# Norming and modulating six of eight first-layer tiles from a second, channel-major copy of the input

## The chip, the cores and the metric

The kernel runs on one core of a Trainium2 chip. The metric is the device time of one launch in microseconds (us), the median of several runs. Before the change three runs took 973.47, 970.46 and 969.55 us, median 970.46 us.

## The reference

Two layers of one mixer each, over 1024 tokens of 1024 channels. Only the head of a layer matters for this change:

```python
def rms_norm(x, gain=None):
    xf = x.astype(jnp.float32)
    y = xf * lax.rsqrt(jnp.mean(xf * xf, axis=-1, keepdims=True) + EPS)
    if gain is not None:
        y = y * gain.astype(jnp.float32)
    return y.astype(x.dtype)

def hybrid_layer(x, c_act, ...):
    mod = c_act @ w_mod + b_mod
    shift, scale, gate = jnp.split(mod[:, None, :], 3, axis=-1)
    h = rms_norm(x, pre_gain) * (1.0 + scale) + shift
    proj = h @ w_in
    ...
    y = jnp.concatenate([a_out, r_out, g_out], axis=-1) @ w_out
    return x + gate * rms_norm(y, post_gain)
```

`proj` is cut into the queries, keys, values and gates of three head groups: windowed attention, retention and gated linear attention. Each token's row of x is divided by its root mean square; each channel is then scaled and shifted.

## The kernel before

**Tiles.** The 1024 tokens are eight tiles of 128. A tile of x is loaded with tokens on partitions, two halves of 128x512. The input projection needs h with channels on partitions, since TensorE contracts over partitions, and in two parts: `hi`, h rounded to the fast 32-bit matmul type, and `lo`, the rest. A projection is 24 products: eight channel blocks, three times (hi by hi, lo by hi, hi by lo), in `accum`. Weights are split in the same way, each unit of 256 columns as four loads of 256 KB into staging buffers, a cast on ScalarE (L488 for the unit `rg`) and a subtraction on VectorE or GpSimd (L491).

**What `pre` does with a tile** of the first layer, from tile 2 on. ScalarE squares both halves and sums (L581). VectorE adds and scales (L534, L528), GpSimd takes the power -1/2 (L529, here "the root"). Both halves are multiplied by the root (L602 on VectorE; L600 on ScalarE for the first half of tiles 2 and 3). TensorE turns them with eight 128x128 transposes by the identity (L176). From PSUM, ScalarE (first half, L622) and VectorE (second half, L624) apply scale and shift, block by block, four each. ScalarE casts each half to `hi` (L628); GpSimd (first half) or VectorE (second half) subtracts for `lo` (L629). Tiles 0 and 1 have a path of their own (`pre_early`), which the change leaves alone.

**Order.** TensorE's order is the program's: generators for each piece of work are resumed by a planner in Python (`pump`, `step`) that keeps a clock of its own and reads latencies from the table `L`. On the other engines and on the DMA queues a scheduler orders the instructions when the program is built; on the chip each engine works its list strictly in order. Almost all loads are issued by SyncE (SP); its eight completion semaphores are used in turn, so a load waits until the eighth load before it has landed.

**Where the change falls.** TensorE's first dense work: the gate unit `gg` for tiles 0 and 1 (272 columns), `rg` for tiles 0 and 1 (256 columns), `gg` for 2 and 3, `rg` for 2 and 3, `gg` for 4 and 5, and so on. Between them stand the transposes of tiles 2 to 7. SyncE at that time loads, in this order: x of tiles 2 and 3, the weights of `rg`, six constants, x of tiles 4 to 7 (L686), small constants, among them the attention sinks (L797, copied by VectorE at L799) and the norm gain `gncol` (L807, scaled by VectorE at L808). VectorE's L1009 finishes the SiLU of a gate after ScalarE's L1007.

The line that the change works on is this one, in `pre`:

```python
            pt = aux()
            for k in range(4):
                transp(pt[:, k * P:(k + 1) * P], xn[j][:, k * P:(k + 1) * P], ident)
```

Of the kernel before, what the change touches and what calls it, by code (L numbers as in the profile page):

```python
# [89 lines left out]
def trunk(ctx: ExitStack, tc: tile.TileContext, ins, cst, out):  # L90
    nc = tc.nc
    V, A, G, T = nc.vector, nc.scalar, nc.gpsimd, nc.tensor
    x_in, c_in, pos_in, w_mod, b_mod, pre_g, post_g, w_in, sinks, gw_in, gb_in, gn_in, w_out = [
        ins[n] for n in _INS
    ]

# [12 lines left out]
    def t2(dt=F32):  # L109
        return gp.tile([P, 512], dt, tag="t2", name=nm("t2"), bufs=B2)  # L110
# [13 lines left out]
    def aux(dt=F32):  # L124
        return ps.tile([P, 512], dt, tag="aux", name=nm("aux"), bufs=8 - MMB)
# [49 lines left out]
    def transp(dst, src, idn):  # L175
        T.transpose(dst, src, idn)  # L176
# [60 lines left out]
    ident = cload("ident", eng=A)  # L237
    ones = cload("ones", eng=A)
# [345 lines left out]
    def pre(l, t, xt, early=False, soon=False):  # L584

        p, tt = divmod(t, 2)
        if tt == 0:
            hT[(l, p)] = place(TOK[l][p])
        h = hT[(l, p)]
        xn = xt if l == 0 and INP else [t2(), t2()]  # L590
        to = [junk, junk] if l == 0 and INP else xn
        r = rstd_early(xt, to) if early and RE or soon and RE2 else rstd2(squares(xt, to))
        rooted[t] = after[2]
        with ExitStack() as es:
            if soon and XF == 3:
                for m in XM:
                    es.enter_context(tc.issue_after(mark[m].ins))
            for j in range(2):
                if EN[f"xn{j}"] == "A" or early and XA[t][j] == "A" or soon and XA[t][j] == "A":
                    A.activation(xn[j], xt[j], AF.Copy, scale=r)  # L600
                else:
                    scaled[t] = V.tensor_scalar(xn[j], xt[j], r, None, ALU.mult)  # L602
        yield 0.5 if early else L["pf1"] if soon else lat("pre1", l)
        if early:
            yield from pre_early(t, xn, h)
            return
        for j in range(2):
            yield (0.0, ("modh", l, j))
            pt = aux()
            for k in range(4):  # L610
                transp(pt[:, k * P:(k + 1) * P], xn[j][:, k * P:(k + 1) * P], ident)
            hf = t2()
            held = ExitStack()
            if soon and (t - 2) in GH:
                for m in gated.get(t - 2, ()):
                    held.enter_context(tc.issue_after(m.ins))
            for k in range(4):
                kt = 4 * j + k
                ks = slice(k * P, (k + 1) * P)
                gain, shift = modc[(l, 1)][:, kt:kt + 1], modc[(l, 0)][:, kt:kt + 1]  # L620
                if TURN[l][j] == "A":
                    A.activation(hf[:, ks], pt[:, ks], AF.Identity, scale=gain, bias=shift)  # L622
                else:
                    V.tensor_scalar(hf[:, ks], pt[:, ks], gain, shift, ALU.mult, ALU.add)  # L624
# [3 lines left out]
            turned[t] = A.activation(hi, hv, AF.Copy)  # L628
            eng(f"hlo{j}").tensor_tensor(lo, hv, f(hi), ALU.subtract)  # L629
            held.close()  # L630
        flag(("hT", l, t), 3.0)
# [871 lines left out]
    while jobs:  # L1503
# [31 lines left out]


# [27 lines left out]
```

## Time and profile before

| | |
|---|---|
| median of three runs | 970.46 us |
| the profiled run, its own time | 971.16 us |
| its span, on which all times below count | 969.4 us |
| granted TensorE clock, mean | 0.996 |
| TensorE without a matmul, 0 to 90 us | 10.6 us |
| TensorE without a matmul, 90 to 960 us | 1.8 us |
| after the last matmul | about 5.8 us |

The fourth to last row and the two below it come from the busy time of TensorE in stretches of 30 us: 20.34, 29.81 and 29.25 us in the first three, and 868.24 of 870 us in the rest up to 960 us. How to read the rows: a timeline row gives start, length, engine, line, operation, output and input, count, and in brackets the idle time before it and what ended it. A row of the chain gives start, length and what the time went to. A row of the stretches gives the length, the busy time of each engine with its count, the granted TensorE clock (1.00 is full), the share of the DMA engines that was busy, and GB/s.

### The profile page before, as it was taken

To read this page: it belongs to the slowest core of one execution; us is meant where nothing else is said; L and a number is where in the kernel's file an instruction comes from. 1 tells how busy PE (TensorE), PEld (TensorE's weight loads), DVE (VectorE), ACT (ScalarE), POOL (GpSimd) and SP (SyncE) were. 2 spreads that over 40 slices of the span, in tenths; PEclk is the share of its full clock that TensorE was granted. 3 is DMA by queue.
4 is the path that set the end of the run, shared out by engine and by line. 5 is a ranking of instruction groups with operands and counts; after the bars stand their busy time and mean duration, and the time that the engine had idled before them with its cause. 6 is when DMAs were issued, how large, how long until landed. Compare 5 with 4: busy or idle time off the path is not lost.

```text
span 969.4 us, 18061 instructions
## 1 busy us (share of the span) xinstructions
PE 951.3 (98%) x6513; PEld 829.4 (86%) x6513; DVE 640.2 (66%) x1525; ACT 410.1 (42%) x1119; POOL 272.5 (28%) x323
## 2 busy tenths in 40 slices
PE   6999999999999999999999999999999999999997
PEld 1799999989998877878889999998999887777886
DVE  6886857777777777655586485686776577763332
ACT  2777312354422666622455531134652166761111
POOL 3243011533430344511242110144423034441000
PEclk9999999999999999999999999999999999999999
DMA  9943314624335355677455160253222333555871
GB/s 313 320 146 110 111 56 129 187 77 112 115 102 150 98 168 180 218 242 237 172 166 172 50 180 22 83 155 92 80 86 77 120 88 105 158 174 174 261 238 65
DMA packets 124293, 140.30 MB, mean 145 GB/s; under 512 B 12734, under 2 KB 95528, under 8 KB 124204
## 3 DMA queue, kind: packets, MB, share of 16 engines
q1 hardware_dynamic: 116204, 127.43, 42.9%
q10 hardware_dynamic: 8000, 11.72, 3.4%
q8 instruction: 51, 0.84, 0.4%
q14 instruction: 38, 0.31, 0.1%
HBM read 102.42 MB, written 34.60 MB: 141 GB/s over the span
## 4 chain that ended last, share of the span: by engine, by line
PE 86%; DMA 7%; DVE 3%; issue 2%; POOL 1%; ACT 0%; SPq 0%; DVEq 0%; ACTq 0%; POOLq 0%
PE mm L161 67%; PE aux L161 15%; PE aux L176 4%; DMA wm<-in_w_mod_dram 2%; DMA t<-in_x_dram 1%; DMA st<-in_w_in_dram 1%; DMA xk<-in_x_dram 1%; DMA t<-aoS 1%; DMA st<-in_w_mod_dram 1%; POOL sm L529 1%; DVE acc L367 0%; DVE t L1292 0%; POOL arena L491 0%; DVE t L624 0%; DMA c_ident<-cst_ident_dram 0%
## 5 line engine op out<-in xcount | busy, mean ns | idle before, releaser
L161 PE MATMUL mm<-arena,arena 128*128 128x256 f32 (+2 forms) x1896 | 303.0, 315 | 1.4 <-ACT arena L628 0.7
L161 PE MATMUL mm<-arena 128*128 128x256 f32 (+2 forms) x1824 | 294.7, 317 | 0.0
L161 PEld LDWEIGHTS mm<-arena,arena 128*128 128x128 f32 x1896 | 261.8, 188 | 24.6 <-ACT arena L628 1.2
L161 PEld LDWEIGHTS mm<-arena 128*128 128x128 f32 x1824 | 255.4, 191 | 22.0 <-issue 1.2
L161 PE MATMUL mm<-arena,mx 128*128 128x512 f32 (+1 forms) x744 | 168.7, 386 | 0.0
L161 PEld LDWEIGHTS mm<-arena,mx 128*128 128x128 f32 x744 | 135.6, 188 | 29.1 <-issue 1.5
L529 POOL TENSOR_TENSOR sm<-sm,mhalf 128x4 f32<-128x4 f32 (+1 forms) x60 | 51.8, 863 | 294.8 <-DVE sm L528 285.3
L491 POOL TENSOR_TENSOR arena<-st,arena 128x512 fp32r<-128x512 f32 x55 | 80.3, 1467 | 91.3 <-ACT arena L145 34.7
L145 ACT ACTIVATE t<-aux 128x512 f32<-128x512 f32 (+1 forms) x96 | 48.7, 521 | 106.4 <-PE aux L176 44.9
L943 POOL TENSOR_TENSOR smx<-smx,sm 128x512 f32<-128x512 f32 x32 | 36.2, 1131 | 114.8 <-DVE sm L942 111.4
L491 DVE TENSOR_TENSOR arena<-st,arena 128x512 fp32r<-128x512 f32 x65 | 62.3, 969 | 4.7 <-PE mm L161 2.6
L145 ACT ACTIVATE arena<-st 128x512 fp32r<-128x512 f32 x82 | 48.5, 626 | 29.0 <-PE mm L161 13.0
L1247 ACT ACTIVATE t<-mm 128x512 f32<-128x512 f32 x30 | 17.9, 597 | 92.2 <-PE mm L161 40.3
L939 ACT ACTIVATE smx<-smx,sm 128x129 f32<-128x129 f32 x128 | 50.0, 393 | 14.0 <-DVE sm L936 13.9
L1248 DVE TENSOR_TENSOR t<-mm,modg 128x512 f32<-128x512 f32 x30 | 20.6, 689 | 48.6 <-ACT t L1247 48.5
L367 DVE SCALAR_TENSOR_TENSOR acc<-st,c_act,acc 128x512 f32<-128x512 f32 x60 | 47.3, 788 | 7.5 <-DMA st<-in_w_mod_dram 6.8
L1292 DVE SCALAR_TENSOR_TENSOR t<-t,sm,t 128x512 f32<-128x512 f32 x32 | 25.9, 846 | 39.7 <-DMA t<-xs 20.8
L176 PE MATMUL aux<-c_ident,t 128*128 128x128 f32 x288 | 45.5, 278 | 2.9 <-DVE t L602 2.9
L176 PEld LDWEIGHTS aux<-c_ident,t 128*128 128x128 f32 x288 | 34.9, 144 | 7.3 <-DVE t L602 4.2
L934 DVE COPY_PREDICATED smx<-c_curmask,aux 128x256 f32<-128x256 int32 x64 | 25.5, 447 | 15.0 <-ACT smx L145 10.4
L990 ACT ACTIVATE t<-aux 128x256 f32<-128x256 f32 x32 | 12.2, 382 | 54.1 <-PE aux L161 26.8
L995 DVE TENSOR_TENSOR t<-aux,sm 128x256 f32<-128x256 f32 x32 | 13.6, 425 | 30.8 <-POOL sm L529 30.8
(214 smaller groups left out, 1300.9 us busy)
## 6 DMA issues: line engine op xcount, KB each, us to landing
st<-in_w_in_dram SPq DMA_DIRECT2D x96, 256.0 KB
st<-in_w_mod_dram SPq DMA_DIRECT2D x64, 256.0 KB
mx<-mixS SPq DMA_DIRECT2D x30, 512.0 KB
mixS<-t SPq DMA_DIRECT2D x64, 128.0 KB
st<-in_w_out_dram SPq DMA_DIRECT2D x32, 256.0 KB
mixS<-t SPq DMA_DIRECT2D x32, 256.0 KB
wm<-in_w_mod_dram SPq DMA_DIRECT2D x12, 512.0 KB
t<-in_x_dram SPq DMA_DIRECT2D x24, 256.0 KB
```

Of the source, the lines that this page charges most:

```text
L145: A.activation(dst, src, AF.Copy)
L161: T.matmul(dst, lhsT, rhs, start=start, stop=stop)
L176: T.transpose(dst, src, idn)
L367: V.scalar_tensor_tensor(acc, wt, c_act[:, k:k + 1], acc, ALU.mult, ALU.add)
L491: i = (G if first == 0 and kc in LOG else V if first == 0 else eng(f"wlo{kc}")).tensor_tensor(wt[:, 1, 2 * kc:2 * kc + 2, 0:256], st, f(hi ...
L529: after[2] = G.tensor_tensor(r, r, mhalf[:, :w], ALU.pow)
L934: V.copy_predicated(sv, curmask.unsqueeze(1).to_broadcast((P, 2, P)), pv[:, :, n // P - 1, :])
L939: A.activation(sm[:, h, :], sm[:, h, :], AF.Exp, bias=mx[:, h:h + 1], accum_out=sums[:, h:h + 1])
L943: eng("pn").tensor_tensor(sm[:, :, 0:128], sm[:, :, 0:128], rs.unsqueeze(2).to_broadcast((P, 4, P)), ALU.mult)
L1247: A.activation(yg, pm, AF.Square, accum_out=ss[:, nh:nh + 1])
L1248: V.tensor_tensor(yg, pm, modg[l][:, 512 * nh:512 * nh + 512], ALU.mult)
L1292: V.scalar_tensor_tensor(xt[j], yg[j], r, xt[j], ALU.mult, ALU.add)
```

## The change

The input is given a second time, as `xt`, laid out on the host as tile, channel in block, block, token, so that a tile can be loaded with channels on partitions. For tiles 2 to 7 of the first layer this copy is loaded (two loads of 256 KB a tile, on SyncE) beside the old one. The old one now only serves the squares, which are written in place. The root belongs to a token, and tokens are now along the free axis; so the root is spread over all partitions by TensorE: GpSimd multiplies the identity by the root (`dg`, a diagonal), and one 128x128 product of a matrix of ones with it gives in each partition the 128 roots. VectorE multiplies both halves with that (PSUM operand, repeated over four blocks). The scale and shift then read SBUF.

```diff
+        turn = l == 0 and t in XTT
+        xn = xt if l == 0 and INP and not turn else [t2(), t2()]
+        if turn:
+            for j in range(2):
+                dma("lxt", xn[j].rearrange("p (k n) -> p k n", k=4), x_t[t, :, 4 * j:4 * j + 4])
+        to = xt if turn else [junk, junk] if l == 0 and INP else xn
         r = rstd_early(xt, to) if early and RE or soon and RE2 else rstd2(squares(xt, to))
...
+            if turn:
+                dg = t1()[:, 0:P]
...
+                    scaled[t] = eng("dg").tensor_scalar(dg, ident, r, None, ALU.mult)
-            for j in range(2):
+            for j in range(0 if turn else 2):
...
+        if turn:
+            pr = aux()
+            mult(pr[:, 0:P], ones, dg, True, True)
+            for j in range(2):
+                xv = xn[j].rearrange("p (k n) -> p k n", k=4)
+                V.tensor_tensor(xv, xv, pr[:, 0:P].unsqueeze(1).to_broadcast((P, 4, P)), ALU.mult)
         for j in range(2):
             yield (0.0, ("modh", l, j))
-            pt = aux()
-            for k in range(4):
-                transp(pt[:, k * P:(k + 1) * P], xn[j][:, k * P:(k + 1) * P], ident)
+            if turn:
+                pt = xn[j]
+            else:
+                pt = aux()
+                for k in range(4):
+                    transp(pt[:, k * P:(k + 1) * P], xn[j][:, k * P:(k + 1) * P], ident)
...
-MIXP = (7,)
+MIXP = (6, 7)
+XTT = (2, 3, 4, 5, 6, 7)
...
-LOG = (0,)
+LOG = (1,)
...
-TT = 7
+TT = 5
...
+    inputs["xt"] = np.asarray(inputs["x"]).reshape(NT, P, KT, P).transpose(0, 3, 2, 1)
```

Besides, some settings change. `hlo0`, the subtraction for the first half's `lo`, goes from GpSimd to VectorE in both layers (`EN`). `LOG` swaps which of the first weight subtractions GpSimd does. `TT` ties the rotation tables to tile 5 instead of 7. `MIXP` lets tile 6 of the last layer load its mixer output into the arena too. Eleven of the planner's latencies in `L` change (tt1 5.71 to 6.3, tt2 6.96 to 3.4, tb1 28.02 to 30.31, mod2 2.4 to 2.3 and in the second layer 2.23 to 2.5, fin1 11.68 to 10.84, lay1 0.05 to 0.49, gz1 and gl1 by up to 0.6).

**TensorE, the first dense products.** `mm_498` and `mm_502` are the product `rg` for tile 0, the `aux` tiles are PSUM banks, `t_59` to `t_65` the normed halves of tiles 2 and 3. Before:

```order
L161 MATMUL mm_498<-arena_356,arena_71 128x256 [waits Activation_49]
L176 MATMUL aux_506<-c_ident,t_59_361 128x128 x4
L176 MATMUL aux_518<-c_ident,t_60_362 128x128 [waits DVE_49]
L176 MATMUL aux_518<-c_ident,t_60_362 128x128 x3
L176 MATMUL aux_530<-c_ident,t_64_373 128x128 [waits Activation_49]
L176 MATMUL aux_530<-c_ident,t_64_373 128x128 x3
L176 MATMUL aux_542<-c_ident,t_65_374 128x128 [waits DVE_49]
L176 MATMUL aux_542<-c_ident,t_65_374 128x128 x3
L161 MATMUL mm_498<-arena_356,arena_71 128x256 x11
```

With the change, at the same place (`t_64` and `t_70` are the diagonals of tiles 2 and 3):

```order
L161 MATMUL mm_502<-arena_356,arena_71 128x256
L161 MATMUL mm_502<-arena_356,arena_71 128x256 [waits Activation_49]
L161 MATMUL aux_510<-t_64_373,c_ones 128x128 [waits Pool_49]
L161 MATMUL aux_528<-t_70_387,c_ones 128x128 [waits Pool_49]
L161 MATMUL mm_502<-arena_356,arena_71 128x256 x9
L161 MATMUL mm_502<-arena_356,arena_71 128x256 [waits DVE_49]
```

Sixteen transposes have become two products with ones. Further on with the change, `mm_804` is `gg` for tile 4 and `mm_871` `gg` for tile 5, `t_124` and `t_140` are the diagonals of tiles 5 and 6:

```order
L161 MATMUL mm_804<-arena_71,arena_356 128x272 [waits DVE_49]
L161 MATMUL mm_804<-arena_71,arena_356 128x272
L161 MATMUL aux_819<-t_124_697,c_ones 128x128 [waits Pool_49]
L176 MATMUL aux_851<-c_ident,sm_653 16x128
L161 MATMUL mm_804<-arena_71,arena_356 128x272 x10
L161 MATMUL aux_872<-t_140_772,c_ones 128x128 [waits Pool_49]
L176 MATMUL aux_890<-c_ident,sm_705 16x128
L161 MATMUL mm_871<-arena_71,arena_356 128x272 [waits Activation_49]
L161 MATMUL mm_871<-arena_71,arena_356 128x272 x3
```

Between tile 5's product with ones and the first product that needs tile 5 stand ten products of tile 4, the product with ones of tile 6 and two small transposes.

**SyncE's loads.** `t_73` to `t_80` are the halves of x of tiles 4 to 7, `sm_437` the sinks. Before, the last loads up to the sinks; the weights of `rg` and six constants were issued ahead of these:

```order
L232 DMA c_qdec<-cst_qdec_dram 128x4 [waits DMAHW3_49]
L686 DMA t_73_401<-in_x_dram 128x512 [waits DMAHW4_49,PE_49]
L686 DMA t_74_402<-in_x_dram 128x512 [waits DMAHW5_49]
L686 DMA t_75_405<-in_x_dram 128x512 [waits DMAHW6_49,PE_49]
L686 DMA t_76_406<-in_x_dram 128x512 [waits DMAHW7_49]
L686 DMA t_77_409<-in_x_dram 128x512 [waits DMAHW0_49,PE_49]
L686 DMA t_78_410<-in_x_dram 128x512 [waits DMAHW1_49]
L686 DMA t_79_413<-in_x_dram 128x512 [waits DMAHW2_49]
L686 DMA t_80_414<-in_x_dram 128x512 [waits DMAHW3_49,PE_49,Activation_49]
L232 DMA c_kdec<-cst_kdec_dram 128x4 [waits DMAHW4_49]
L232 DMA c_cdt<-cst_cdt_dram 128x2 [waits DMAHW5_49]
L797 DMA sm_437<-in_attn_sinks_dram 128x16 [waits DMAHW6_49]
```

With the change, `t_59` to `t_66` are the second copy of tiles 2 and 3, and `st_389` to `st_401` the weights of `rg`:

```order
L150 DMA t_59_361<-in_xt_dram 128x512 [waits DMAHW2_49,DVE_49]
L150 DMA t_60_362<-in_xt_dram 128x512 [waits DMAHW3_49,DVE_49,PE_49]
L150 DMA t_65_375<-in_xt_dram 128x512 [waits DMAHW4_49,DVE_49,PE_49]
L150 DMA t_66_376<-in_xt_dram 128x512 [waits DMAHW5_49,DVE_49,PE_49]
L150 DMA st_389<-in_w_in_dram 128x2x256 [waits DMAHW6_49]
L150 DMA st_393<-in_w_in_dram 128x2x256 [waits DMAHW7_49,DVE_49]
L150 DMA st_397<-in_w_in_dram 128x2x256 [waits DMAHW0_49,Pool_49]
L150 DMA st_401<-in_w_in_dram 128x2x256 [waits DMAHW1_49,DVE_49]
```

Four loads of `xt` now stand ahead of the four of `rg`. Seven loads of x follow these at once, and then, from the sixth of them on (`t_80`, `t_81`, and `sm_441` for the sinks):

```order
L705 DMA t_80_414<-in_x_dram 128x512 [waits DMAHW7_49]
L705 DMA t_81_417<-in_x_dram 128x512 [waits DMAHW0_49]
L232 DMA c_causal<-cst_causal_dram 128x128 [waits DMAHW1_49]
L232 DMA c_mask_423<-cst_mask_dram 128x128 [waits DMAHW2_49]
L232 DMA c_curmask<-cst_curmask_dram 128x128 [waits DMAHW3_49]
L232 DMA c_rmask<-cst_rmask_dram 128x256 [waits DMAHW4_49]
L232 DMA c_hmask<-cst_hmask_dram 128x4 [waits DMAHW5_49]
L232 DMA c_qdec<-cst_qdec_dram 128x4 [waits DMAHW6_49]
L232 DMA c_kdec<-cst_kdec_dram 128x4 [waits DMAHW7_49]
L232 DMA c_cdt<-cst_cdt_dram 128x2 [waits DMAHW0_49]
L816 DMA sm_441<-in_attn_sinks_dram 128x16 [waits DMAHW1_49]
```

All eight constants now stand behind the x loads, and the load of the sinks waits for the eighth load before it, `c_causal`, which itself stands behind the seventh load of x.

**VectorE, around the copy of the sinks.** `t_93_523` is the second half of tile 2 after scale and shift; `sink` are the sinks. Before:

```order
L624 TENSOR_SCALAR t_93_523<-aux_518,mod_11_120,mod_10_119 128x128 [waits PE_49]
L1009 SCALAR_TENSOR_TENSOR t_88_495<-t_87_493,mm_320 128x256 [waits Activation_49]
L624 TENSOR_SCALAR t_93_523<-aux_518,mod_11_120,mod_10_119 128x128 x2
L799 COPY sink_436<-sm_437 128x8 [waits DMAHW6_49]
L799 COPY sink_436<-sm_437 128x8
L624 TENSOR_SCALAR t_93_523<-aux_518,mod_11_120,mod_10_119 128x128
L907 COPY smx_3981<-sink_436 128x4 [waits DVE_49]
L907 COPY smx_3998<-sink_436 128x4
```

With the change that half is `t_94`, made from the loaded copy `t_60`, and `t_93_514` is the first half:

```order
L528 TENSOR_SCALAR sm_631<-sm_629 128x1 [waits DVE_49]
L818 COPY sink_440<-sm_441 128x8 [waits DMAHW1_49]
L818 COPY sink_440<-sm_441 128x8
L1028 SCALAR_TENSOR_TENSOR t_99_565<-t_98_563,mm_502 128x256 [waits Activation_49]
L926 COPY smx_3956<-sink_440 128x4 [waits DVE_49]
L926 COPY smx_3973<-sink_440 128x4
L643 TENSOR_SCALAR t_94_521<-t_60_362,mod_11_120,mod_10_119 128x128 [waits Activation_49]
L643 TENSOR_SCALAR t_94_521<-t_60_362,mod_11_120,mod_10_119 128x128 x2
L648 TENSOR_TENSOR arena_71<-t_93_514,arena_71 128x4x128 [waits Activation_49]
L643 TENSOR_SCALAR t_94_521<-t_60_362,mod_11_120,mod_10_119 128x128
```

Before, three of the four blocks of tile 2's second half stood ahead of the copy of the sinks; now all four stand behind it, and the subtraction for the first half too.

More of the change, by code (lines that the diff above doesn't have):

```diff
@@ L92, in trunk @@
     V, A, G, T = nc.vector, nc.scalar, nc.gpsimd, nc.tensor
-    x_in, c_in, pos_in, w_mod, b_mod, pre_g, post_g, w_in, sinks, gw_in, gb_in, gn_in, w_out = [
+    x_in, c_in, pos_in, w_mod, b_mod, pre_g, post_g, w_in, sinks, gw_in, gb_in, gn_in, w_out, x_t = [
         ins[n] for n in _INS
@@ L589, in pre @@
         h = hT[(l, p)]
-        xn = xt if l == 0 and INP else [t2(), t2()]
-        to = [junk, junk] if l == 0 and INP else xn
+        turn = l == 0 and t in XTT
[4 more added lines that the diff above has]
+        to = xt if turn else [junk, junk] if l == 0 and INP else xn
         r = rstd_early(xt, to) if early and RE or soon and RE2 else rstd2(squares(xt, to))
@@ L597, in pre @@
                     es.enter_context(tc.issue_after(mark[m].ins))
-            for j in range(2):
+            if turn:
+                dg = t1()[:, 0:P]
+                if EN["dg"] == "A":
+                    scaled[t] = A.activation(dg, ident, AF.Copy, scale=r)
+                else:
+                    scaled[t] = eng("dg").tensor_scalar(dg, ident, r, None, ALU.mult)
+            for j in range(0 if turn else 2):
                 if EN[f"xn{j}"] == "A" or early and XA[t][j] == "A" or soon and XA[t][j] == "A":
@@ L606, in pre @@
             return
+        if turn:
[4 more added lines that the diff above has]
+                V.tensor_tensor(xv, xv, pr[:, 0:P].unsqueeze(1).to_broadcast((P, 4, P)), ALU.mult)
         for j in range(2):
             yield (0.0, ("modh", l, j))
-            pt = aux()
-            for k in range(4):
-                transp(pt[:, k * P:(k + 1) * P], xn[j][:, k * P:(k + 1) * P], ident)
+            if turn:
+                pt = xn[j]
+            else:
+                pt = aux()
+                for k in range(4):
+                    transp(pt[:, k * P:(k + 1) * P], xn[j][:, k * P:(k + 1) * P], ident)
             hf = t2()
@@ L1533 @@
 _INS = ["x", "c", "positions", "w_mod", "b_mod", "pre_norm_gain", "post_norm_gain", "w_in", "attn_sinks",
-        "gla_gate_w", "gla_gate_b", "gla_norm_gain", "w_out"]
+        "gla_gate_w", "gla_gate_b", "gla_norm_gain", "w_out", "xt"]
 def kernel(**inputs):
```

4 lines of the change are left out of this document (2 added, 2 removed).

## The prediction

> **What bounds the kernel now.** I began with the page: busy shares, then the slices.
>
> ```profile
> PE 951.3 (98%) x6513; PEld 829.4 (86%) x6513; DVE 640.2 (66%) x1525; ACT 410.1 (42%) x1119; POOL 272.5 (28%) x323
> PE   6999999999999999999999999999999999999997
> DMA  9943314624335355677455160253222333555871
> ```
>
> TensorE is the bound, in every slice but the ends. The DMA engines are full only in the first two slices, up to 48 us, and the change puts its new transfers there. So two questions count: how much work TensorE loses, and whether it comes to wait in the first 90 us. Next, TensorE's waits, longest first:
>
> ```profile
> PE aux L176 <- DVE posr L408: 6.2, 1, 6.2
> PE aux L176 <- DVE t L602: 2.9, 2, 2.5
> PE mm L161 <- ACT arena L628: 0.7, 2, 0.5
> ```
>
> (Total, times, longest.) The first two lie ahead of 20 us, before anything that the change touches, and stay. The third is the wait for tile 5; more below. After 90 us TensorE stands still for 1.8 us in all, so the later settings (`MIXP`, `TT`, the subtraction moved off GpSimd, most latencies) have almost nothing to win; I cost them at nothing, hidden under TensorE's products, 1.8 us at most.
>
> **The change part by part.** *TensorE's work.* The timeline of TensorE at the transposes:
>
> ```profile
> 43.69 2.07 PE L176 MATMUL aux<-c_ident,t 128*128 128x128 f32 x16
> 45.52 4.91 PE L161 MATMUL mm<-arena,arena 128*128 128x256 f32 x41
> 50.26 2.81 PE L161 MATMUL mm<-arena 128*128 128x272 f32 x21
> 58.17 1.04 PE L176 MATMUL aux<-c_ident,t 128*128 128x128 f32 x8
> 58.96 3.91 PE L161 MATMUL mm<-arena,arena 128*128 128x256 f32 x31
> 62.71 1.04 PE L176 MATMUL aux<-c_ident,t 128*128 128x128 f32 x8
> 63.51 1.47 PE L161 MATMUL mm<-arena,arena 128*128 128x256 f32 x10
> 67.43 0.77 PE L161 MATMUL mm<-arena,arena 128*128 128x272 f32 x4 [0.21 <-ACT arena L628]
> 68.73 0.65 PE L161 MATMUL mm<-arena,arena 128*128 128x272 f32 x3 [0.54 <-ACT arena L628]
> 69.22 1.03 PE L176 MATMUL aux<-c_ident,t 128*128 128x128 f32 x8
> 70.10 0.27 PE L176 MATMUL aux<-c_ident,sm 128*16 128x128 f32 x1
> 70.12 2.38 PE L161 MATMUL mm<-arena,arena 128*128 128x272 f32 x17
> 72.34 0.99 PE L161 MATMUL mm<-arena 128*128 128x256 f32 x7
> 73.17 1.03 PE L176 MATMUL aux<-c_ident,t 128*128 128x128 f32 x8
> 73.97 5.15 PE L161 MATMUL mm<-arena 128*128 128x256 f32 x41
> ```
>
> From start to next start the 48 transposes hold TensorE for 1.83 + 0.79 + 0.80 + 0.88 + 0.80 = 5.10 us. In their place come six full-precision 128x128 products. By shape:
>
> ```profile
> L161 PE MATMUL aux<-mx,mx 128*128 128x128 f32 x192 | 24.0, 275 | 0.0
> L161 PE MATMUL aux<-t,t 128*128 128x128 f32 x56 | 9.3, 288 | 0.0
> ```
>
> The code issues 96 products of the first kind and 28 of the second, so each is two rows: 24.0/96 = 0.25 us and 9.3/28 = 0.33 us. I take the nearer, 0.25, for 1.5 us in all; ends 0.6 (each as dear as a transpose, 0.10) and 2.0. Net **-3.6 us**.
>
> *The weights of `rg` come later.* From the chain of waits:
>
> ```profile
> 34.91 5.33 DMA st<-in_w_in_dram
> 48.67 2.06 DMA gncol<-in_gla_norm_gain_dram
> ```
>
> The last `rg` weights landed at 40.24. Now four loads of `xt`, 4 x 256 KB = 1.05 MB, stand ahead. The stretch in which they would move:
>
> ```profile
> 36.00:38.00 2.00, 2.00 (x11) 2.00 (x10) 1.98 (x7) 1.98 (x6) 0.24 (x1) 0.50 1.10 351
> 42.28 1.14 ACT L488 ACTIVATE arena<-st 128x512 fp32r<-128x512 f32 x2
> ```
>
> At 351 GB/s that is 3.0 us: landing at 43.2. ScalarE casts the last part in 0.63, so at 43.85 instead of 43.42 (second row): most of the delay is hidden by ScalarE's own lateness, and TensorE's seventh product loses **+0.4 us**. At the 387 GB/s of the stretch at 22 us (below) it is 0.1, at the 266 of 19 us 1.3. `gg` of tile 2 (50.26 before) then starts at 50.26 - 1.83 + 0.5 + 0.4 = 49.3.
>
> *The sinks, and what is queued behind them.* VectorE's timeline around the copy, and ScalarE's cast:
>
> ```profile
> 46.23 0.41 DVE L1009 SCALAR_TENSOR_TENSOR t<-t,mm 128x256 f32<-128x256 f32 x1
> 48.42 0.47 DVE L799 COPY sink<-sm 128x8 f32<-128x8 f32 x2 [1.15 <-DMA sm<-in_attn_sinks_dram]
> 48.81 0.40 DVE L624 TENSOR_SCALAR t<-aux,mod,mod 128x128 f32<-128x128 f32 x1
> 49.13 0.23 DVE L907 COPY smx<-sink 128x4 f32<-128x4 f32 x2
> 49.24 0.63 ACT L628 ACTIVATE arena<-t 128x512 fp32r<-128x512 f32 x1 [1.47 <-DVE t L624]
> 49.91 0.69 DVE L629 TENSOR_TENSOR arena<-t,arena 128x512 fp32r<-128x512 f32 x1 [0.24 <-ACT arena L628]
> 70.41 0.88 DVE L602 TENSOR_SCALAR t<-t,sm 128x512 f32<-128x512 f32 x2 [0.39 <-POOL sm L529]
> ```
>
> Already before, VectorE stood 1.15 us for the sinks, which nobody needs yet; the second half of tile 2 was cast by 49.87, just in time for 50.26. Now the sinks' load is issued only when `c_causal` has landed, behind seven x loads: 1.84 MB at 351 GB/s after 43.2 is 48.4. Issue 0.4 and 2.06 us to land (the row of `gncol`, a small load too) give 50.9. Behind the waiting copy stand all of tile 2's second half and its first subtraction. From start to start in the rows: copies 0.39, small copies 0.14; L1009 0.4, subtraction 0.6 (0.69 with its start-up). The four blocks now read SBUF: 0.40 each is the PSUM price; L602 (the row at 70.41) does four times as much from SBUF in 0.44. I take 0.2, 0.8 for four. Together 2.3, so 53.2, and the cast (0.63) ends at 53.8. TensorE has done four products of tile 2 by 49.8 and waits **+4.0 us**. Ends: at 387 GB/s the sinks land at 50.2 and the wait is 3.5; at 266, with blocks at 0.40, they land at 53.6 and it is 6.6. Below the first end lies a rival, no wait at all.
>
> *The granted clock.* After TensorE's one long wait before:
>
> ```profile
> 17.67 0.55 PE L176 MATMUL aux<-c_ident,t 128*128 128x128 f32 x3 [2.52 <-DVE t L602]
> 18.00:19.00 1.00, 0.77 (x8) 0.95 1.09 361
> 19.00:20.00 1.00, 0.87 (x4) 0.50 1.33 266
> 22.00:23.00 1.00, 1.00 (x4) 0.85 1.05 387
> ```
>
> (TensorE busy, clock, DMA share, GB/s.) The rows at 20 and 21 us read 0.50 too. So a wait of 2.52 us was followed by some 3.4 us at half clock, 0.05 + 3 x 0.50 + 0.15 = 1.7 us lost. A wait of 4 us should bring the same, a little of it while TensorE still stands: **+1.5 us**, ends 0 and 3.4 (two such stretches). The Trainium skill, "TensorE: Matmul & The Clock Gate", section "HAM oscillation — how this bites in real kernels", warns of TensorE gaps above about 3.4 us; by that the 4 us wait costs clock as well, and the sum is the same, while a wait just below it would be free. The trace does not bear out so sharp a limit, since 2.52 us sufficed.
>
> *Tile 5.* Its chain now starts with the product with ones; then one multiply (0.69, below), four blocks (1.47), a cast (0.63, above), and hand-overs of 0.2 in all: 3.0 us.
>
> ```profile
> L1248 DVE TENSOR_TENSOR t<-mm,modg 128x512 f32<-128x512 f32 x30 | 20.6, 689 | 48.6 <-ACT t L1247 48.5
> 69.95 1.47 ACT L622 ACTIVATE t<-aux,mod,mod 128x128 f32<-128x128 f32 x4
> ```
>
> TensorE has ten products (0.13 each by the row at 70.12), tile 6's 0.25 and a small transpose of 0.1 to cover it, 1.65 us: a wait of 1.35 where 0.75 stood (67.43, 68.73), **+0.6 us**; ends -0.75 and +1.5. Tile 4 has all 24 products of `rg` 3 (0.12 each, row 73.97) for the same chain, 2.9 us: nothing, at most 0.6. Tiles 6 and 7 have over 5 us. GpSimd's diagonal and the roots for tiles 4 to 7 end long before they are asked for.
>
> **Sum:** -3.6 + 0.4 + 4.0 + 1.5 + 0.6 = +2.9 us. The profiled run took 971.16 (span 969.4), 0.7 above the median of 970.46; so 974.1 for a profiled run, **973.4** for the median.
>
> **The rivals.** *No wait for the sinks.* They land before about 47, or tile 2 does not hang on them; then neither wait nor half clock: -3.6 + 0.4 + 0.6 = -2.6, **967.9**. For it: before, they came 1.15 us after VectorE asked, and VectorE now asks later, with four multiplies ahead. Against: their issue waits for a landing behind seven x loads, whatever the rate; even at 387 GB/s that alone is 47.7.
>
> *The clock stays low.* After the wait at tile 2 the gate does not open after one stretch: TensorE meets tile 5's wait soon after. Two more stretches of 1.7 us give +2.9 + 3.4 = +6.3, **976.8**, slower than before; it decides if the clock is still 0.50 some 4 us after TensorE resumes. For it: the stretch from 36 us above shows 0.50 while TensorE was busy throughout. Against: at 22 us it opened after one stretch.
>
> *The wait is too short for the gate:* it is at its lower end, 3.5 us, and the clock stays full, as it did through the waits of 0.21 and 0.54 us at 67 to 69 us: -1.5 - 0.5 from the sum, +0.9, **971.4**. Against: the wait of 2.52 us. This is how the skill's limit of about 3.4 us, in "TensorE: Matmul & The Clock Gate", would have it for a slightly shorter wait.
>
> *It does not do what it says:* the reordered rest takes all 1.8 us of later waits, tile 5 waits no more (-0.75) and tile 2 not either: -3.6 + 0.4 - 0.75 - 1.8 = -5.8, **964.7**, the most it could win.
>
> **How the numbers follow.** Forecast 0.50, no wait 0.22, clock stays low 0.16, short wait 0.07, the last 0.05. The forecast's own ends, each with the other terms as taken: 970.5 (no wait at tile 5, 3.5 at tile 2, 0.6 products) to 977.0 (1.3 for `rg`, 6.6 at tile 2). The range reaches from a little under the second case, by the cheaper products, to the forecast's upper end: 967.0 to 977.0. A measurement here can tell about 0.5%, 4.85 us, from no change. Faster by that needs every wait gone and more: 0.06. Slower: the clock case and the upper end of the forecast, 0.22. Same: 0.72.
>
> **What would show it.** In the new profile: no transposes of tiles 2 to 7 and six products of some 0.25 us; a wait of VectorE for the sinks until about 51 us; behind it a TensorE wait of about 4 us ended by the cast of tile 2 near 53.8; granted clock 0.50 for about 3.4 us around it; a wait of about 1.4 us at tile 5. It would be wrong if VectorE copies the sinks before 48, or if a wait over 1 us appears after 90 us.

## The result, and the profile after

| | before | after |
|---|---|---|
| median (runs) | 971.43 us (17) | 975.67 us (17) |
| lowest to highest | 969.45 to 973.47 | 973.38 to 979.32 |
| profiled execution, its span | 971.16, 969.4 | 973.9, 972.2 |
| start of `gg` for tile 6 in the profile | 78.95 | 82.71 |

The ratio of after to before is 1.0045, 95% interval 1.0037 to 1.0054: about 4.2 us slower, where the forecast was 973.4 us, 2.9 us slower, with a range of 967 to 977. By the bound of 0.5% set in the prediction this is "same", just inside it, though the interval leaves out a ratio of 1: the change is a little slower.

Shares and slices on the page of after:

```profile
PE 946.8 (97%) x6477; PEld 825.1 (85%) x6477; DVE 640.9 (66%) x1541; ACT 410.4 (42%) x1117; POOL 256.3 (26%) x315
PE   5989999999999999999999999999999999999997
DMA  9973414533335355777555160353222323555861
```

TensorE's wait that grew (total, times, longest):

```profile
PE mm L161 <- ACT arena L647: 5.3, 3, 3.2
```

TensorE is busy for 4.5 us less (946.8 for 951.3), and the time is longer all the same. The timeline of TensorE (start, duration; in brackets the idle time ahead of the row and what ended it):

```profile
43.97 0.72 PE L161 MATMUL aux<-t,c_ones 128*128 128x128 f32 x4
44.45 2.01 PE L161 MATMUL mm<-arena,arena 128*128 128x256 f32 x15
46.72 3.55 PE L161 MATMUL mm<-arena,arena 128*128 128x256 f32 x26 [0.25 <-POOL arena L491]
50.10 0.66 PE L161 MATMUL mm<-arena 128*128 128x272 f32 x4
53.93 5.18 PE L161 MATMUL mm<-arena 128*128 128x272 f32 x27 [3.17 <-ACT arena L647]
67.89 2.19 PE L161 MATMUL mm<-arena,arena 128*128 128x272 f32 x14 [0.55 <-ACT arena L647]
69.92 0.38 PE L161 MATMUL aux<-t,c_ones 128*128 128x128 f32 x2
70.17 1.51 PE L161 MATMUL mm<-arena,arena 128*128 128x272 f32 x10
73.62 3.29 PE L161 MATMUL mm<-arena,arena 128*128 128x272 f32 x24 [1.61 <-ACT arena L647]
82.71 6.17 PE L161 MATMUL mm<-arena,arena 128*128 128x272 f32 x48
```

The two products with ones of tiles 2 and 3 hold TensorE for 0.48 us, from 43.97 to 44.45. `gg` for tile 2 begins at 50.10, does four products and stands for 3.17 us; tiles 4 and 5 wait 0.55 and 1.61. What ended the long wait, on VectorE and then on ScalarE:

```profile
50.75 0.25 DVE L818 COPY sink<-sm 128x8 f32<-128x8 f32 x2 [2.95 <-DMA sm<-in_attn_sinks_dram]
51.38 0.85 DVE L643 TENSOR_SCALAR t<-t,mod,mod 128x128 f32<-128x128 f32 x3
53.27 0.61 ACT L647 ACTIVATE arena<-t 128x512 fp32r<-128x512 f32 x1
```

VectorE stands 2.95 us for the sinks, does tile 2's blocks behind them, and ScalarE casts that half until 53.88. The clock after it (us; TensorE, its weight loads, VectorE, ScalarE, GpSimd busy; granted clock; DMA share; GB/s):

```profile
55.00:56.00 1.00, 1.00 (x8) 1.00 (x7) 0.39 (x1) 1.00 (x4) 0.00 (x0) 0.68 0.64 137
56.00:57.00 1.00, 1.00 (x6) 1.00 (x6) 1.00 (x3) 0.36 (x2) 0.00 (x0) 0.50 1.00 337
57.00:58.00 1.00, 1.00 (x7) 1.00 (x6) 0.41 (x2) 0.28 (x2) 0.00 (x0) 0.50 0.96 273
58.00:59.00 1.00, 1.00 (x8) 0.97 (x7) 0.95 (x2) 1.00 (x3) 0.00 (x0) 0.61 0.93 264
```

0.32 + 0.50 + 0.50 + 0.39 = 1.7 us lost. The stretch that holds the whole turned path, before and then after:

```profile
38.00:80.00 42.00, 41.08 (x331) 39.96 (x330) 32.73 (x82) 34.92 (x94) 16.86 (x16) 0.98 0.50 153
```

```profile
38.00:80.00 42.00, 35.96 (x264) 33.74 (x263) 29.34 (x79) 32.68 (x86) 13.15 (x16) 0.96 0.69 222
```

TensorE stands 6.0 of these 42 us where it stood 0.9, and the DMA engines are busy at 0.69 instead of 0.50. So far the profile reads as the prediction did, but for what TensorE loses at the weights of `rg` (more below). It does not say what would happen if the sinks came in time.

### The profile page after: what moved, and what is told of

It is laid out like the page before. It is cut to its first block, busy times and chain, and to the rows that moved or that the text cites. A ratio compares the mean times of both kernels' runs of the same rounds, so it can differ in the third digit from the quotient of the medians.

```text
span 972.2 us, 18020 instructions
## 1 busy us (share of the span) xinstructions
PE 946.8 (97%) x6477; PEld 825.1 (85%) x6477; DVE 640.9 (66%) x1541; ACT 410.4 (42%) x1117; POOL 256.3 (26%) x315
## 4 chain that ended last, share of the span: by engine, by line
PE 86%; DMA 6%; DVE 3%; ACT 2%; issue 1%; SPq 1%; POOL 1%; DVEq 0%; ACTq 0%; POOLq 0%
PE mm L161 67%; PE aux L161 15%; PE aux L176 4%; DMA st<-in_w_in_dram 2%; DMA wm<-in_w_mod_dram 1%; DMA t<-in_x_dram 1%; DMA xk<-in_x_dram 1%; DVE t L1311 1%; DMA mx<-in_x_dram 1%; ACT t L641 0%; POOL arena L491 0%; SPq L318 0%; DMA mixS<-t 0%; ACT t L581 0%; DMA c_ident<-cst_ident_dram 0%
## 5 line engine op out<-in xcount | busy, mean ns | idle before, releaser
L161 PE MATMUL mm<-arena,arena 128*128 128x256 f32 (+2 forms) x1944 | 315.1, 317 | 3.5 <-ACT arena L647 2.2
L161 PEld LDWEIGHTS mm<-arena,arena 128*128 128x128 f32 x1944 | 271.2, 188 | 30.0 <-ACT arena L647 2.6
L161 PE MATMUL mm<-arena,mx 128*128 128x512 f32 (+1 forms) x696 | 157.7, 385 | 0.0
L161 PEld LDWEIGHTS mm<-arena,mx 128*128 128x128 f32 x696 | 126.6, 188 | 26.8 <-issue 1.2
L491 POOL TENSOR_TENSOR arena<-st,arena 128x512 fp32r<-128x512 f32 x55 | 79.8, 1458 | 129.2 <-ACT arena L145 73.9
L491 DVE TENSOR_TENSOR arena<-st,arena 128x512 fp32r<-128x512 f32 x65 | 61.3, 955 | 6.1 <-PE mm L161 2.4
L176 PE MATMUL aux<-c_ident,t 128*128 128x128 f32 x240 | 38.2, 274 | 2.7 <-DVE t L612 2.7
L176 PEld LDWEIGHTS aux<-c_ident,t 128*128 128x128 f32 x240 | 28.7, 142 | 7.0 <-DVE t L612 3.9
```

Of the source, the lines that this page charges most:

```text
L161: T.matmul(dst, lhsT, rhs, start=start, stop=stop)
L491: i = (G if first == 0 and kc in LOG else V if first == 0 else eng(f"wlo{kc}")).tensor_tensor(wt[:, 1, 2 * kc:2 * kc + 2, 0:256], st, f(hi ...
```

## Experiments

Theory S: the sinks hold tile 2, and their wait and its half clock are the loss. The rivals: the later settings; a second chain that is nearly as late; the added transfers as such; the longer chain of each turned tile. Ratios are to the kernel before on the same chip.

### E1 and E2: the sinks loaded early, after and before

```diff
-    sinkn = small(16)
-    nc.sync.dma_start(sinkn, sinks...)
...
+    sinkn = cp.tile([P, 16], F32, name="sinkn")
+    A.dma_start(sinkn, sinks...)
     xm = mix_tile(F32)...
```

> The changed kernel with the load of the sinks moved ahead of the x loads (issued on ScalarE's queue in the first microseconds, into a tile of its own); nothing else. Theory (VectorE's wait for the sinks holds tile 2's second half, TensorE waits 3.17 us for it and runs some 3 us at half clock after it): VectorE does not wait for the sinks, TensorE's wait at tile 2 is below 0.3 us, no half clock at 55 to 59 us, and the time falls by 3.2 + 1.7 = 4.9 us, from 975.7 to about 970.8, a ratio to the kernel before of 0.999. If only the wait costs and the clock does not come back: 972.5, 1.001. Rival 1 (the transfers of xt and the late weights hold TensorE anyway, another wait takes the place): about 975, 1.004. Rival 2 (the loss lies in the later settings): no change, 975.7, 1.0045.

> The control: the kernel before with the same move of the sinks' load. VectorE waited 1.15 us for them there but TensorE did not wait for VectorE at tile 2. Theory: VectorE's wait goes, the time does not change, ratio 1.000 within 0.0007. If an early load by itself is worth something, E1's gain has to be cut by it.

E1: 976.07 us, ratio 1.0046 (1.0033 to 1.0058), nothing gained. E2: 1.0005 (0.9995 to 1.0015), no change. TensorE in E1, then VectorE, then SyncE:

```profile
52.72 3.67 PE L161 MATMUL mm<-arena 128*128 128x272 f32 x27 [1.09 <-ACT arena L647]
67.47 3.22 PE L161 MATMUL mm<-arena,arena 128*128 128x272 f32 x14 [2.84 <-ACT arena L647]
...
50.16 0.86 DVE L643 TENSOR_SCALAR t<-t,mod,mod 128x128 f32<-128x128 f32 x3 [0.86 <-ACT t L641]
...
58.99 0.89 SPq L150 DMA_DIRECT2D t<-in_xt_dram  x2
```

The wait at tile 2 fell from 3.17 to 1.09 us, and its half clock went. But tile 4, which had waited 0.55, now waits 2.84, and three slices behind it stand at 0.50; its `xt` was issued at 58.99, in the change from 56.27 on. Theory S names a true wait and predicts the wrong time for its removal: it falls. TensorE goes on at tile 2 at 52.72 for 53.93, so a second chain ends only 1.2 us ahead of the one through the sinks; which one was the next question.

### E3 and E4: the turned path alone, the settings alone

E3 is the changed kernel with the latencies, `hlo0`, `MIXP`, `LOG` and `TT` of before; E4 is the changed kernel with `XTT = ()`.

> The turned path alone (second layout, products with ones), with all the settings of the kernel before (latencies, the subtraction of hlo0 on GpSimd, MIXP, LOG, TT). Theory (the settings cost and win nothing): as the changed kernel, ratio 1.0045 within 0.0015, with a TensorE wait of 2.5 to 4 us at tile 2. Rival (a part of the loss or of the cover comes from the settings): a ratio off by more than 0.002, below 1.0025 or above 1.0065.

> The changed kernel's settings with no turned tile (the transposes stay for tiles 2 to 7). Theory (settings are worth nothing): ratio 1.000 within 0.001, no wait above 1 us at tile 2. Rival (the settings themselves cost, by the subtraction of tile 2's first half on VectorE ahead of the second half, or later): 1.002 to 1.004.

E4: 971.56 us, 1.0003 (0.9995 to 1.0012): alone the settings are worth nothing. E3: 978.4 us, 1.0074 (1.0056 to 1.0093): without them the turned path loses more, by 0.0029 or 2.8 us, and the intervals of E3 and of the change just do not meet. Two waits of E3 that the change does not have:

```profile
59.20 1.40 PE L161 MATMUL mm<-arena 128*128 128x272 f32 x9 [0.84 <-DVE arena L648]
69.31 1.06 PE L161 MATMUL mm<-arena,arena 128*128 128x272 f32 x6 [0.41 <-POOL arena L648]
```

The second is the subtraction of the first half, left on GpSimd in E3: with the turned path there is no longer time for it there. These waits are not what E3 loses most by, though. At tile 6 it is only 0.7 us behind the change (83.40 for 82.71), at the end of the span 4.7 (976.9 for 972.2). Behind tile 6 TensorE waits 1.86 us at 193.99 us where the change waits 0.66, and runs at half clock from 195 to 199. Which of the settings prevents this was not tried.

### E5 to E8: more buffers, earlier products

The twelve buffers of 128x512 now hold `xt` of tiles 2 and 3 while eight x loads want one. E5 is E1 with fourteen, E6 the changed kernel with fourteen, E7 the kernel before with fourteen, and E8 is E5 with the products with ones of tiles 4 to 7 earlier:

```diff
-B2, B1, BS, BST, MMB, SMB = 12, 8, 11, 5, 3, 6
+B2, B1, BS, BST, MMB, SMB = 14, 8, 11, 5, 3, 6
...
-L = {... "pre1": 7.43, ...}      # E8 only
+L = {... "pre1": 4.5, ...}
```

> E1 (early sinks) with 14 buffers of 128x512 in place of 12. In E1 the wait at tile 2 fell from 3.17 to 1.09 us and one of 2.84 at tile 4 came up; VectorE's blocks of tile 2 began only behind ScalarE's L641 (0.86 us), and SyncE's eighth x load stood 1.7 us for a buffer, with every later load behind it. Theory A (a second chain, the ring of twelve buffers, now holding four xt tiles, eight x tiles and the outputs of the blocks, stands beside the sinks; taking away both frees TensorE): the wait at tile 2 is below 0.3 us, xt of tile 4 is issued some 2 us earlier, the wait at tile 4 is about 1 us, no half clock behind; 971 to 972.5, ratio 1.000 to 1.002. Theory B (SyncE's order alone, xt of tile 4 behind stores and four weight loads): tile 4 waits over 2 us again, 974.5 to 976, ratio 1.004 to 1.005.

> The changed kernel with 14 buffers, the sinks' load where the change left it. If the sinks hold tile 2 by themselves: VectorE waits for them until about 51 us, TensorE's wait at tile 2 stays 2.5 to 3.5 us, 974 to 976, ratio 1.003 to 1.005. If the ring alone was it: as E5.

> The control: the kernel before with 14 buffers. TensorE had no wait there above 0.6 us after 20 us, so both theories give no change, ratio 1.000 within 0.001.

> E5 with the planner's latency ahead of the products with ones of tiles 4 to 7 cut from 7.43 to 4.5, so that they stand 12 to 24 products of TensorE earlier ahead of the tile that needs them. Theory (tile 5 waits 1.4 to 1.6 us for a chain of 3.0 us behind its product with ones, covered by only 1.65): that wait falls below 0.5 us and the time by 1 to 1.5 us against E5, if xt and the roots are there by then. If xt or the roots come too late, TensorE waits at the product itself, and nothing is won or 1 us lost.

E5: 975.83 us, 1.0039 (1.0026 to 1.0051). E6: 975.15, 1.0034 (1.0021 to 1.0047). E7: 971.56, 1.0003 (0.9993 to 1.0013). E8: 976.09, 1.0046 (1.0032 to 1.006). TensorE at tiles 2 and 4 in E5, then SyncE:

```profile
51.79 4.19 PE L161 MATMUL mm<-arena 128*128 128x272 f32 x31 [0.42 <-ACT arena L647]
67.53 2.69 PE L161 MATMUL mm<-arena,arena 128*128 128x272 f32 x14 [3.37 <-ACT arena L647]
...
54.77 3.45 SPq L150 DMA_DIRECT2D st<-in_w_in_dram  x4
58.31 0.89 SPq L150 DMA_DIRECT2D t<-in_xt_dram  x2
```

With both chains gone tile 2 waits 0.42 us: the buffers, or what stood behind them, were the second chain there. In E6, with the sinks late, VectorE stood 4.08 us for them and TensorE 3.45 at tile 2, so the sinks do hold tile 2 by themselves. But in E5 all of it comes back at tile 4, and the time is theory B's; whether its cause, the late `xt`, is right, E9 tests. E8, tiles 4 and 5:

```profile
66.73 2.93 PE L161 MATMUL mm<-arena,arena 128*128 128x272 f32 x21 [3.10 <-ACT arena L647]
71.42 2.47 PE L161 MATMUL mm<-arena,arena 128*128 128x272 f32 x17 [0.57 <-ACT arena L647]
```

The earlier product took tile 5's wait down from 1.61 in the change, 0.92 in E5, to 0.57, about as expected, but the median did not fall with it (the profiled run, 973.63, is the fastest of the six). Tile 4 kept 3.10: there it is not the product that is late.

One moment hardly moves in most of these. TensorE goes on with tile 4 at 67.89 us in the change, and at 67.47, 67.61, 67.53 and 66.73 in E1, E3, E5 and E8 (E6, which leaves tile 2 only at 55.43, does so at 69.86). What is won at tile 2 is mostly waited for at tile 4.

### E9 and E10: `xt` of tiles 4 to 7 on ScalarE's queue

```diff
-                dma("lxt", xn[j]..., x_t[...])
+                dma("lxt" if t < 4 else "lxt4", xn[j]..., x_t[...])   # "lxt4": ScalarE
```

> E5 (early sinks, 14 buffers) with the xt loads of tiles 4 to 7 issued on ScalarE's queue in place of SyncE's, where in E5 they stood behind four stores and four weight loads (issued at 58.3 us, TensorE's wait for tile 4 3.37 us). Theory A (the late xt of tile 4 is the third chain): issued before 50 us, the wait at tile 4 falls below 1 us, no half clock behind it, 970.5 to 972.5, ratio 0.999 to 1.001. Theory B (VectorE's own queue holds tile 4: the cast and the low halves of the next weights, L147 and L491, stand between or ahead of its two multiplies, and wait for weight loads that SyncE issues just as late): the wait at tile 4 stays above 2 us, 974 to 976, ratio 1.003 to 1.005.

> E9 with the earlier products of E8 (latency 4.5), which puts tile 4's multiplies and blocks ahead of the cast and the low halves of the next weights on VectorE. Theories A and B both: the wait at tile 4 is gone (below 0.5 us). Tile 5's multiplies still stand behind the two L491 on VectorE: if the weights have landed by 60 us, no wait above 1 us is left and the time is that of fewer products alone, 968 to 970.5, ratio 0.997 to 0.999; if VectorE stands for the weights, tile 5 waits 1 to 3 us and the time is 971 to 974, ratio 1.000 to 1.003.

E9: 976.56 us, 1.0050 (1.0033 to 1.0067). E10: 980.03, 1.0088 (1.0072 to 1.0104), the slowest of all. In E9 ScalarE's queue, VectorE, TensorE:

```profile
53.13 0.34 ACTq L150 DMA_DIRECT2D t<-in_xt_dram  x1
...
60.94 0.69 DVE L622 TENSOR_TENSOR t<-t,aux 128x512 f32<-128x512 f32 x1 [1.50 <-PE aux L161]
62.96 0.43 DVE L147 CAST arena<-st 128x512 fp32r<-128x512 f32 x1 [1.33 <-DMA st<-in_w_in_dram]
64.23 0.68 DVE L622 TENSOR_TENSOR t<-t,aux 128x512 f32<-128x512 f32 x1
...
67.28 0.96 PE L161 MATMUL mm<-arena,arena 128*128 128x272 f32 x4 [3.58 <-ACT arena L647]
```

`xt` of tile 4 now goes out 5 us earlier (not before 50 us, as theory A wanted), and its first multiply follows the product at once, so `xt` is no longer what comes last. The second stands behind a cast of the next weights, for whose landing VectorE waits 1.33 us. In E10 the multiplies stand ahead of that cast, and TensorE waits for something else again, a result bank that VectorE empties (L1028) behind the same cast:

```profile
62.62 0.43 DVE L147 CAST arena<-st 128x512 fp32r<-128x512 f32 x1 [2.08 <-DMA st<-in_w_in_dram]
...
66.30 3.87 PE L161 MATMUL mm<-arena,arena 128*128 128x272 f32 x21 [2.10 <-DVE t L1028]
```

So theory B of E9 held in its wait, with a time just above its range; E10, at 980.03, lies above what both theories allowed. Four different last arrivals were taken away in turn (sinks, buffers, `xt`, the order on VectorE), and the time stayed or rose. The weights of E9 and E10 were issued at 58.7 and 59.1 us, in E5 at 54.77, behind two stores that took SyncE 3.8 us to issue in E9 and E10; why these took so long was not tried.

### E11: the transfers alone, in the kernel before

```diff
-        to = [junk, junk] if l == 0 and INP else xn
+        to = xt if soon else [junk, junk] if l == 0 and INP else xn
+        if soon:
+            for j in range(2):
+                nc.sync.dma_start(xn[j], x_in[0, t * P:(t + 1) * P, 512 * j:512 * j + 512])
```

> The kernel before with nothing of the change but the traffic: four loads of 256 KB on SyncE's queue at the place of the four xt loads, into the buffers that the scaled tiles 2 and 3 are written to later. The squares of tiles 2 and 3 are written over x as in the change, so those two tiles come out with other values; the instructions and their number stay. Theory T (the loads fill a stretch in which the DMA engines are full, and everything behind them on SyncE, x, constants, sinks, stores and the next weights, comes some 3 us later; whichever wait is taken away, the next late load takes over, as in E1, E5, E9 and E10): VectorE copies the sinks at about 51 us, TensorE waits 2 to 4 us at tile 2 or 4, with or without half clock, and the time rises by 3 to 7 us, ratio 1.003 to 1.007. Theory C (the longer chain of each turned tile on VectorE and ScalarE is what holds TensorE): at most 0.5 us for the later weights of rg, ratio 1.000 to 1.001.

976.6 us, ratio 1.0058 (1.0041 to 1.0075): 5.6 us for four loads that nobody reads. TensorE, then VectorE:

```profile
43.51 1.02 PE L161 MATMUL mm<-arena,arena 128*128 128x256 f32 x4 [1.61 <-ACT arena L488]
45.28 1.10 PE L161 MATMUL mm<-arena,arena 128*128 128x256 f32 x3 [0.75 <-ACT arena L488]
85.05 6.17 PE L161 MATMUL mm<-arena,arena 128*128 128x272 f32 x48
...
54.09 0.25 DVE L802 COPY sink<-sm 128x8 f32<-128x8 f32 x2 [3.72 <-DMA sm<-in_attn_sinks_dram]
```

One slice of the clock, as above:

```profile
50.00:51.00 1.00, 1.00 (x7) 1.00 (x6) 0.36 (x2) 1.00 (x3) 0.11 (x1) 0.50 0.62 166
```

`gg` for tile 6 begins 6.1 us later than before (78.95). The size is theory T's; the places are not. TensorE did not wait at tile 2: it came late itself, by 2.4 us at the weights of `rg` and by a half clock from 44 to 52 us (0.24 + 6 x 0.50 + 0.17 = 3.4 us lost). ScalarE's casts of those weights stood behind the scaling of tile 2 there (first at 42.85, before at 39.01), so a part of this is an order that moved with the loads, and the run does not divide the two.

### E12: only tiles 4 to 7 turned

```diff
-XTT = (2, 3, 4, 5, 6, 7)
+XTT = (4, 5, 6, 7)
```

> The changed kernel with only tiles 4 to 7 turned (one line; tiles 2 and 3 keep their transposes, and need no load of xt ahead of 48 us). 32 transposes go (about 3.3 us) and four products of 0.25 us come: -2.3 us on TensorE. Theory T: SyncE's queue is as before, no wait above 0.6 us at tile 2, waits at tiles 4 and 5 as in the kernel before (0.75 us) or up to 1.5 us: 968.5 to 970.5, ratio 0.9975 to 0.999, better than both kernels. Theory C: the turned tiles 4 and 5 hold TensorE for 2 us or more whatever the traffic: 971 to 974, ratio 1.000 to 1.003.

974.69 us, 1.0040 (1.0024 to 1.0056). TensorE:

```profile
69.70 2.04 PE L161 MATMUL mm<-arena,arena 128*128 128x272 f32 x14 [1.23 <-ACT arena L647]
78.91 6.16 PE L161 MATMUL mm<-arena,arena 128*128 128x272 f32 x48
97.88 2.67 PE L161 MATMUL mm<-arena,arena 128*128 128x256 f32 x21 [2.76 <-DVE t L1028]
```

Neither theory's account holds. Tiles 2 and 4 do not wait, tile 5 waits 1.23 us, as theory T had it, and by tile 6 the kernel stands even with the one before, its 2.3 us of saved work used up on the way, by a wait of 1.50 us for the weights of `rg` (at 43.66) and a half clock from 45 to 49 us among others. Then it loses 2.76 us at a place where the kernel before does not wait, for a result bank that VectorE empties late. The time is in theory C's range, though not by C's mechanism. No version tried beats the kernel before.

## Why the prediction was right, and where it was not

- **TensorE's work, -3.6.** Right. The six products cost 0.48 for two, then 0.14 to 0.22 from their start to the next (69.92 to 70.17 is 0.25 with a small transpose inside): about 1.2 in all, for 1.5 taken; so -3.9.
- **`rg`'s weights, +0.4.** Too small. The cast part is right: ScalarE ends the casts at 43.70 (forecast 43.85). But with the transposes saved `gg` of tile 2 should start at 50.26 - 1.83 + 0.48 = 48.91, and it starts at 50.10: +1.2. The listed waits, 0.65 us for 0.15 before, are only a part of that, and vary by themselves (1.50 in E4 and E7, which have no load of `xt`). GpSimd now makes the diagonals of tiles 2 and 3 (L607) before it subtracts for the low halves of these weights (L491). Its last subtraction ends at 46.67, before at 44.76; TensorE stands for it at 46.72 and starts 14 products from 46 to 48 us, where before it started 24. E3, with `LOG` as before, stands for the same subtraction (0.31 us), so that setting is not the reason. The sum has no term for those two diagonals. Before, then after:

```profile
43.49 1.27 POOL L491 TENSOR_TENSOR arena<-st,arena 128x512 fp32r<-128x512 f32 x1
```

```profile
43.06 1.09 POOL L607 TENSOR_SCALAR t<-c_ident,sm 128x128 f32<-128x128 f32 x1
44.13 2.54 POOL L491 TENSOR_TENSOR arena<-st,arena 128x512 fp32r<-128x512 f32 x2
```

- **The sinks, +4.0.** The mechanism was right to 0.2 us: copied at 50.75 (forecast 50.9), the cast done at 53.88 (53.8). The wait was 3.17, because TensorE reached tile 2 at 50.10 and not at 49.3. So the two errors cancel: 1.2 + 3.2 is the forecast's 0.4 + 4.0, since what is lost at `rg` is not waited for at the sinks.
- **Half clock, +1.5.** 1.7 in the profile. The mean granted clock over all runs fell from 0.9966 (the 23 runs of before in E1's comparison) to 0.9946 (17 of after), 0.002 of 972 us or, as an estimate, 1.9 us. The profiled pair as a whole does not show this fall (0.996 and 0.997): before has half-clock stretches of its own at 19 and 36 us, ahead of the weights of `rg`.
- **Tile 5, +0.6; tile 4, up to 0.6.** 1.61 for 0.75, +0.86; tile 4 0.55.
- **The sum, +2.9.** The two profiled executions differ by 2.7; the medians by 4.2. The terms as measured make -3.9 + 1.2 + 3.2 + 1.7 + 0.9 + 0.55 = +3.6 for +3.8 at tile 6. About 1 us is won back behind tile 6 in this pair; that was not traced to a row.

Two statements behind the number were wrong. The rival "no wait for the sinks" said that without it neither wait nor half clock remains, 967.9 us. E1 took that wait away and gave 976.07. The prediction's "tile 4: nothing, at most 0.6" held only because tile 2's wait gave tile 4 its time; with tile 2 freed, tile 4 waited 2.84 to 3.58 us (E1, E5, E8, E9) and TensorE went on there at most 1.2 us earlier. And the settings were costed "at nothing": so they are alone (E4), but they save the turned path 2.8 us (E3), mostly behind tile 6.

What the transfers cost by themselves is less clear than the sum's near hit suggests. Its terms that come from them, 0.4 + 4.0 + 1.5 = 5.9 us, stand beside 5.6 in E11, but E11 pays at other places, in part by an order on ScalarE that moved, so that the two agree may be chance. And E12, without the early transfers, still loses 3.9 us, mostly elsewhere. So it is shown that four early loads added to the kernel before cost more than the whole loss, that a version without them loses nearly as much as the change, that the sinks hold tile 2 in the change (E6), and that freeing tile 2 wins nothing. How the loss divides between late transfers, the longer chain and instructions that change places on VectorE, ScalarE and GpSimd is open. That the forecast came within 1.3 us of the difference is in part luck: two of its errors cancel, and the wait that it named could go without any gain.

## What to carry to other kernels

A wait that the profile names is only the last arrival. Before crediting its removal, look for the second-latest on the engines in front; here, with VectorE and ScalarE busy for 70% and 78% of the stretch, the wait came back two tiles on. Price moved bytes by adding the loads alone to the old kernel: here that one run showed a loss of the size to be explained, while five kernels that removed single waits gained nothing. Then look where that run pays, since it need not be where the change does. Settings that are worthless alone can be what a new path stands on, so measure them in its company.

## What the runs showed of the hardware

Half clock did not follow from the length of a wait. After a wait of 2.76 us in E3 and one of 3.10 in E8 (row above) the clock stayed at 1.00; after 2.84 in E1 and 3.17 in the change it fell to 0.50 for some 3 us, after 3.58 in E9 for about twice that. It fell as well after 1.50 us in E12 (45 to 49 us) and after 1.86 in E3 (195 to 199 us). The stretch from 36 us that the prediction quotes at 0.50 in before, with TensorE busy, stands at 1.00 in after. E3, at the wait, then E9, six us after TensorE resumed at 67.28:

```profile
53.00:54.00 1.00, 0.14 (x1) 0.14 (x2) 0.56 (x3) 0.82 (x2) 0.00 (x0) 1.00 0.45 124
54.00:55.00 1.00, 1.00 (x9) 1.00 (x10) 1.00 (x4) 1.00 (x4) 0.00 (x0) 1.00 0.51 171
56.00:57.00 1.00, 1.00 (x10) 1.00 (x9) 0.07 (x1) 0.96 (x4) 0.78 (x1) 1.00 0.95 300
```

```profile
73.00:74.00 1.00, 1.00 (x6) 1.00 (x6) 1.00 (x5) 1.00 (x4) 0.00 (x0) 0.50 0.30 25
```

The prediction used a wait of 2.52 us to say that waits of this size bring half clock. The Trainium skill, "TensorE: Matmul & The Clock Gate", "Part 1: The HAM clock gate", says that the window over which activity is judged runs freely and does not start with the kernel's work, so that the same kernel can meet it at another phase. That agrees with waits of 1.5 to 3.2 us falling on either side here, while the limit of about 3.4 us that the prediction quoted from it is not one these runs show: 2.84 us was enough in E1.

VectorE and GpSimd slowed each other in the subtraction of the weights (L491). In E5 VectorE's first took 0.68 us, and GpSimd's, begun 0.02 us after it, 1.82, where it takes 1.27 in the row of before above. VectorE's second took 1.72 and ended 0.55 us after GpSimd's. The times, rough as they are on GpSimd, read as if one engine stood while the other worked; no run tries this by itself:

```profile
62.15 0.68 DVE L491 TENSOR_TENSOR arena<-st,arena 128x512 fp32r<-128x512 f32 x1
62.82 1.72 DVE L491 TENSOR_TENSOR arena<-st,arena 128x512 fp32r<-128x512 f32 x1
...
62.17 1.82 POOL L491 TENSOR_TENSOR arena<-st,arena 128x512 fp32r<-128x512 f32 x1
```
